# Both halves of a doubling stage asked for before its evictions, in the block inverse of a hybrid layer

## The chip, the cores and the metric

One Trainium2 chip, one core, one launch. The metric is the device time of the whole kernel in microseconds; the kernel before has a median of 1342.84 us over three runs (1340.01 to 1342.85).

The engines are named as in the profile: PE is TensorE (matmuls), PEld its weight loads, DVE VectorE, ACT ScalarE, POOL GpSimd, SP SyncE, whose queue issues most DMAs. L1113 means line 1113 of the kernel before.

## The reference, cut to what matters

A transformer layer over 512 tokens of width 1024: a projection, two sequence mixers (A: gated delta rule with 8 heads; B: retention with 4 heads), an output projection and an MLP. The change lies in mixer A. There, for each head and each chunk of tokens, the inverse of a unit lower triangular matrix is needed:

```
lower = jnp.where(strict, jnp.einsum('bhncd,bhnmd->bhncm', k_beta, k) * decay, 0.0)
eye = jnp.broadcast_to(jnp.eye(CHUNK, dtype=jnp.float32), lower.shape)
t_inv = lax.linalg.triangular_solve(lower, eye, left_side=True, lower=True, unit_diagonal=True)
u = jnp.einsum('bhncm,bhnme->bhnce', t_inv, v * beta[..., None])
w = jnp.einsum('bhncm,bhnmd->bhncd', t_inv, k_beta * jnp.exp(g_cum)[..., None])
...
def step(state, inp):
    qe, ww, uu, aqk, kd, ld = inp
    v_new = uu - jnp.einsum('bhck,bhkv->bhcv', ww, state)
    o = jnp.einsum('bhck,bhkv->bhcv', qe, state) + jnp.einsum('bhcm,bhmv->bhcv', aqk, v_new)
    state = state * ld[..., None, None] + jnp.einsum('bhck,bhcv->bhkv', kd, v_new)
    return state, o
```

## The kernel before, in words

Most of the kernel is large matrix products in three terms (weights and activations are each split into a high and a low part). Weights come by DMA into a `raw` tile, ACT makes the high part `whi` (L148) and DVE the low part `wlo` (L149); then PE multiplies.

The kernel uses chunks of 128 tokens for mixer A, so there are 8 heads x 4 chunks = 32 triangular blocks of 128 x 128. They are inverted in two steps.

*Base inverse* (`base_inverse`, L1032). The 32 x 32 diagonal blocks of all 32 matrices are inverted by substitution on DVE. ACT then copies these inverses to their places in `rt` in eight copies (L1077) and one copy within `rn` (L1071). `rn` holds the inverses in one orientation, `rt` in the other.

*Doubling* (`double_blocks`, L1080). It makes 64 x 64 inverses out of pairs of 32 x 32 ones, then 128 x 128 out of 64 x 64. The 32 matrices are two groups of 16. A 32 x 32 pair has two corners, at partitions 0 to 63 and 64 to 127 (`pairs`).

- Stage 1 (`first`) multiplies a block of the matrix (`mt`, a view of the tile `acc`) by `rn`, into a PSUM bank for each group (`p1`); the result is evicted to `ys` (a view of the tile `mrb`), which stage 2 reads.
- Stage 2 (`left`, `right`) multiplies `ys` by `rt`, into a bank for each group (`p2`); the result is evicted, negated, to `rt` and to `rn`. `rn` is read by the third stage, `rt` by the stages from the fourth on.
- The third and fourth products work on 64 x 64 blocks in quarters of the set, and the change leaves them alone.

In each of the first two stages a loop over q issues one corner of group 0 abreast with the other corner of group 1 (L1110, L1118; in stage 2 also one `right` product), then the evictions of these corners, then the next q. The evictions of stage 1 are L1113 on DVE for group 0 and L1114 on ACT for group 1; those of stage 2 are L1123 (ACT) and L1125 (DVE) into `rt`, and L1127, on DVE for both groups, into `rn`. Each matmul here is float32, and the profile shows two PE records (and two weight loads) for it: 64 in a half of stage 1, 96 in a half of stage 2. PSUM banks come from a pool of three under the tag `dl`.

The order of PE's work is fixed by hand: a planner (`Clock`, L659) interleaves "chains" (dependent work such as the doubling) with "fillers" (the large products). A chain gives the planner a pause with `yield`, in microseconds of the planner's own clock; until it is due, fillers are placed, in units of three matmuls of 0.227 us each by the planner (L753 to L758). Every matmul goes through L668 and keeps program order. After the doubling the event "doubled" is done, and four recurrences follow, which hand over between PE and ACT or DVE in each of four chunks. `DB_US` is 1.2. The order on the other engines is set by a scheduler, by priorities; the evictions here have `KEY_PRIO` (600), the splits of weights in this phase `AHEAD` (700), L1077 has 0.

SP issues the loads of weights; some loads are followed by copies and accumulating DMAs (L135, by POOL) that prepare sums of weight blocks in DRAM for later.

Of the kernel before, what the change touches and what calls it, by code (L numbers as in the profile page):

```python
# [15 lines left out]
ALU = mybir.AluOpType  # L16
# [13 lines left out]
SMALL_US, CONV_US, TOK_US, PK_US, INV_US, DB_US = 10.5, 6.5, 2.5, 2.0, 46, 1.2  # L30
VT_US, KS_US, PX_US, PC_US, GATE_US, FEAT_US, INV_PRIO, CONV_PRIO, SMALL_PRIO, KEY_PRIO, DECAY_US, AHEAD, TR_US, REC_PRIO, OUT_PRIO, SUM_PRIO = 2.5, 2.4, 3.5, 2.4, 11.0, 1.0, 0, 600, 800, 600, 20.0, 700, 2.2, 900, 900, 300
# [32 lines left out]
def hybrid_block_kernel(ctx: ExitStack, tc: tile.TileContext, a: dict, out: bass.AP):  # L64
    nc = tc.nc
# [379 lines left out]
    def two_halves(pool, name, tag, n, width):  # L445
        return Halves(n, [
            pf.tile([P, 2048], F32, tag=tag, name=name)[:, : n * width].rearrange("p (n w) -> p n w", n=n),
            pool.tile([P, n, width], F32, name=name),
        ])
# [5 lines left out]
    rt = two_halves(pa, "rt", "f2", 16, P)  # L455
# [6 lines left out]
    with tc.tile_pool(name="xp", bufs=2) as xp:  # L462
# [105 lines left out]
        hi, lo = kept[0]  # L568
# [359 lines left out]
    def acc_rows(t, half):  # L928
        return acc_t[:, t, half * 512 : half * 512 + 512]
# [54 lines left out]
    with delta_rule:  # L984
# [95 lines left out]
        def double_blocks():  # L1080
            groups = [(m0, slice(m0, m0 + 16), rn_all[0][:, m0 : m0 + 16, :]) for m0 in (0, 16)]
            ys = [rn_all[1][:, h, :].rearrange("p (n c) -> p n c", n=16) for h in (1, 0)]
            pairs = [(slice(b, b + 32), slice(b + 32, b + 64)) for b in (0, 64)]

            def bank(n):
                return psx.tile([P, T], F32, tag="dl", name="dl", bufs=3).rearrange("p (n c) -> p n c", n=n)

            def abreast(*streams):

                for step in zip(*streams):  # L1090
                    before = clock.now
                    for args in step:
                        clock.matmul(*args, start=True, stop=True)
                    clock.now = before + (clock.now - before) / len(streams)

            def first(g, q, p):
                (m0, _, rn), (lo, hi) = groups[g], pairs[q]
                return [(p[hi, n, :], mt[lo, m0 + n, hi], rn[lo, n, 0:32]) for n in range(16)]

            def left(g, q, p):  # L1100
                (m0, _, _), (lo, hi) = groups[g], pairs[q]
                return [(p[lo, n, :], ys[g][hi, n, 0:32], rt[hi, m0 + n, hi]) for n in range(16)]

            def right(g, p):
                m0, hi = groups[g][0], pairs[0][1]
                return [(p[hi, n, :], rt[hi, m0 + n, hi], ys[g][hi, n, 0:32]) for n in range(16)]

            p1 = [bank(16) for _ in range(2)]
            for q in range(2):
                abreast(first(0, q, p1[0]), first(1, 1 - q, p1[1]))  # L1110
                with tc.high_priority(KEY_PRIO):
                    hi0, hi1 = pairs[q][1], pairs[1 - q][1]
                    nc.vector.tensor_copy(ys[0][hi0, :, 0:32], p1[0][hi0])  # L1113
                    nc.scalar.copy(ys[1][hi1, :, 0:32], p1[1][hi1])  # L1114
            yield 1.5 * DB_US
            p2 = [bank(16) for _ in range(2)]
            for q in range(2):
                abreast(left(0, q, p2[0]), left(1, 1 - q, p2[1]), right(q, p2[q]))  # L1118
                with tc.high_priority(KEY_PRIO):
                    for g, (lo, hi) in ((0, pairs[q]), (1, pairs[1 - q])):  # L1120
                        dst = rt[lo, groups[g][1], hi]
                        if g:
                            nc.scalar.mul(dst, p2[g][lo], -1.0)  # L1123
                        else:
                            nc.vector.tensor_scalar(dst, p2[g][lo], -1.0, None, ALU.mult)  # L1125
                    hi = pairs[0][1]
                    nc.vector.tensor_scalar(groups[q][2][hi, :, 0:32], p2[q][hi], -1.0, None, ALU.mult)  # L1127
            yield 1.5 * DB_US
            lo, hi = slice(0, 64), slice(64, 128)
            units = [(g, slice(8 * i, 8 * i + 8)) for g in range(2) for i in range(2)]  # L1130

            def third(u, p):
                g, ns = units[u]
                m0, _, rn = groups[g]
                return [(p[hi, n - ns.start, :], mt[lo, m0 + n, hi], rn[lo, n, :]) for n in range(ns.start, ns.stop)]

            def fourth(u, p):
                g, ns = units[u]
                m0 = groups[g][0]
                return [(p[lo, n - ns.start, :], ys[g][hi, n, :], rt[hi, m0 + n, hi]) for n in range(ns.start, ns.stop)]  # L1140

            def keep_third(u, p):
                g, ns = units[u]
                with tc.high_priority(KEY_PRIO):
                    nc.vector.tensor_copy(ys[g][hi, ns], p[hi])

            def keep_fourth(u, p):
                g, ns = units[u]
                m0 = groups[g][0]
                with tc.high_priority(KEY_PRIO):  # L1150
                    nc.scalar.mul(rt[lo, m0 + ns.start : m0 + ns.stop, hi], p[lo], -1.0)

            for u in range(2):
                p = bank(8)
                abreast(third(u, p))
                keep_third(u, p)
            yield 1.5 * DB_US
            for u in range(2):
                p3, p4 = bank(8), bank(8)
                abreast(third(2 + u, p3), fourth(u, p4))  # L1160
                keep_third(2 + u, p3)
                keep_fourth(u, p4)
                yield 1.5 * DB_US
            for u in range(2, 4):
                p = bank(8)
                abreast(fourth(u, p))
                keep_fourth(u, p)
            yield 1.5 * DB_US
            clock.done("doubled")
# [268 lines left out]
        def delta_chain():  # L1438
            yield "inverse"
            yield from double_blocks()  # L1440
            for g2 in range(4):
                for f in range(4):
                    yield f"v{g2}{f}"
                yield f"q{g2}"
                yield from recurrence(g2)
                clock.start(gate_chain(g2))
                if g2 == 1:
                    feature_sums()
# [55 lines left out]
    with tc.tile_pool(name="pb", bufs=1) as pb_:  # L1504
# [129 lines left out]
        for h in range(4):  # L1634
# [13 lines left out]
            else:  # L1648
                for half, pss in branch_partial(w_br[1], og, 4 * (h - 1)):
                    for t in range(4):  # L1650
                        dst = acc_rows(t, half)
# [381 lines left out]
```

## Time and profile before

| what | value |
|---|---|
| median of three runs | 1342.84 us |
| profiled execution | 1337.54 us |
| its span, first to last instruction | 1335.8 us |
| DVE busy | 70% |
| ACT busy | 50% |
| mean granted PE clock | 0.992 |

The profile is of one execution, so sums are made against its 1337.54 us, of which 1335.8 are the span. Rows of the timeline give start and length in us, engine, line, operation, the tile written and those read, and in brackets the idle time before the group and what released it. In rows of stretches each engine has its busy time and its count of instructions; PEclk is the share of the PE clock that was granted. "issue" is idle time for which the profile knows no releaser.

### The profile page before, as it was taken

Reading aid. Unit: us, or ns where it says so; the run is one execution under the profiler, and the core shown is the slowest. Engines: PE = TensorE matmul, PEld = TensorE weight load, DVE = VectorE, ACT = ScalarE, POOL = GpSimd, SP = SyncE. Lnnn points to the kernel's source line nnn. Section 1 sums busy time; section 2 is a strip of 40 time slices with the busy share of each in tenths; the row PEclk is TensorE's granted clock in tenths of the full one; section 3 lists DMA queues with packets and bytes.
Section 4 is the critical chain, followed back from the end, with each engine's and each line's share of the span. In section 5 each row is a group of like instructions: output and inputs, shape, how many; then the busy total and the mean of one; then the engine's idle time right before and its main releaser. Section 6 shows DMA issues by size and latency. Waiting matters only on the chain.

```text
span 1335.8 us, 17525 instructions
## 1 busy us (share of the span) xinstructions
PE 1310.9 (98%) x6591; PEld 1089.5 (82%) x6591; DVE 930.7 (70%) x1561; ACT 668.0 (50%) x1167; POOL 90.4 (7%) x95
## 2 busy tenths in 40 slices
PE   9999799999999999999999999999999999999997
PEld 7888588888888878888888888888889888888786
DVE  6889556676567568987577766889675746647478
ACT  5784345555534434554453353455356636355364
POOL 2101100000010001000000000000001010000001
PEclk9999799999999999999999999999999999999999
DMA  5436935366766658896394282455629796848835
GB/s 192 132 110 158 190 80 126 95 146 177 191 166 159 139 158 172 248 290 137 76 274 112 80 239 77 134 169 175 231 77 236 224 250 172 252 130 228 230 116 136
DMA packets 115557, 223.16 MB, mean 167 GB/s; under 512 B 6982, under 2 KB 38896, under 8 KB 114960
## 3 DMA queue, kind: packets, MB, share of 16 engines
q1 hardware_dynamic: 96496, 175.13, 41.2%
q0 software_dynamic: 16944, 40.54, 18.6%
q10 hardware_dynamic: 2032, 6.36, 1.3%
q8 instruction: 52, 0.85, 0.3%
q14 instruction: 33, 0.27, 0.1%
HBM read 216.75 MB, written 72.37 MB: 216 GB/s over the span
## 4 chain that ended last, share of the span: by engine, by line
PE 86%; DVE 6%; ACT 4%; DMA 2%; issue 1%; DVEq 0%; ACTq 0%
PE mm L668 17%; PE mm L317 17%; PE dl L317 11%; PE mm L93 10%; PE mm L94 10%; PE mm L95 10%; PE dl L668 6%; PE tr L397 1%; DVE wlo L149 1%; PE dl L94 1%; PE dl L95 1%; PE dl L93 1%; PE tr L677 1%; DMA raw<-sums 1%; PE mm L632 1%
## 5 line engine op out<-in xcount | busy, mean ns | idle before, releaser
L149 DVE TENSOR_TENSOR wlo<-raw,whi 128x1024 fp32r<-128x1024 f32 x269 | 328.2, 1222 | 210.4 <-ACT whi L148 206.2
L148 ACT CAST whi<-raw 128x1024 fp32r<-128x1024 f32 x269 | 282.4, 1052 | 358.2 <-PE mm L317 73.1
L668 PE MATMUL mm<-actT,whi 128*128 128x512 f32 x448 | 145.9, 407 | 0.0
L317 PE MATMUL mm<-whi,xsum 128*128 128x512 f32 x384 | 120.6, 390 | 0.0
L95 PE MATMUL mm<-hn,wlo 128*128 128x512 f32 (+1 forms) x288 | 105.4, 366 | 0.0
L94 PE MATMUL mm<-hn,whi 128*128 128x512 f32 (+1 forms) x288 | 105.3, 366 | 0.0
L93 PE MATMUL mm<-hn,whi 128*128 128x512 f32 (+1 forms) x288 | 105.3, 366 | 0.0
L668 PEld LDWEIGHTS mm<-actT,whi 128*128 128x128 f32 x448 | 82.7, 192 | 15.5
L668 PE MATMUL mm<-actT,wlo 128*128 128x512 f32 x224 | 88.9, 397 | 0.0
L317 PEld LDWEIGHTS mm<-whi,xsum 128*128 128x128 f32 x384 | 71.8, 188 | 14.9
L317 PE MATMUL mm<-wlo,xsum 128*128 128x512 f32 x192 | 74.8, 390 | 0.0
L317 PE MATMUL dl<-whi,ffq 128*128 128x512 f32 x224 | 71.2, 389 | 0.0
L668 PE MATMUL mm<-whi,og 128*128 128x512 f32 x192 | 62.7, 398 | 0.0
L93 PEld LDWEIGHTS mm<-hn,whi 128*128 128x128 f32 x288 | 54.3, 189 | 8.8
L94 PEld LDWEIGHTS mm<-hn,whi 128*128 128x128 f32 x288 | 54.3, 189 | 8.7
L95 PEld LDWEIGHTS mm<-hn,wlo 128*128 128x128 f32 x288 | 54.3, 189 | 8.6
L317 PE MATMUL dl<-whi,actT 128*128 128x512 f32 x192 | 61.2, 390 | 0.0
L668 PE MATMUL mm<-whi,actT 128*128 128x512 f32 x176 | 59.9, 403 | 1.0 <-DVE qf L906 1.0
L317 PE MATMUL mm<-whi,ffq 128*128 128x512 f32 x192 | 60.9, 389 | 0.0
L135 POOL DMA_DIRECT2D sums<-in_w_in_dram x28 | 32.6, 1164 | 386.9 <-DMA sums<-in_w_in_dram 386.9
L1826 DVE TENSOR_TENSOR ffq<-r,ffq 128x512 fp32r<-128x512 f32 (+1 forms) x64 | 39.1, 620 | 28.1 <-ACT ffq L1826 27.9
L93 PE MATMUL mm<-actT,whi 128*128 128x512 f32 x128 | 51.5, 403 | 0.0
(393 smaller groups left out, 2840.9 us busy)
## 6 DMA issues: line engine op xcount, KB each, us to landing
raw<-in_w_in_dram SPq DMA_DIRECT2D x95, 512.0 KB, 4.8
raw<-sums SPq DMA_DIRECT2D x64, 512.0 KB, 4.2
raw<-in_w_up_dram SPq DMA_DIRECT2D x36, 512.0 KB, 7.0
sums<-in_w_in_dram SPq DMA_DIRECT2D x32, 512.0 KB, 5.3
sums<-in_w_down_dram SPq DMA_DIRECT2D x32, 512.0 KB, 6.4
sums<-in_w_in_dram POOLq DMA_DIRECT2D x28, 512.0 KB, 7.2
raw<-in_w_down_dram SPq DMA_DIRECT2D x24, 512.0 KB, 4.5
sums<-sums POOLq DMA_DIRECT2D x20, 512.0 KB, 8.1
```

The lines of the kernel that those rows point to most:

```text
L93: nc.tensor.matmul(ps, lh, rh, start=first, stop=False)
L94: nc.tensor.matmul(ps, lh, rl, start=False, stop=False)
L95: nc.tensor.matmul(ps, ll, rh, start=False, stop=last)
L135: tc.keep_in_program_order(nc.gpsimd.dma_start(dst, src, accum_op=ALU.add))
L148: nc.scalar.copy(hi[:, :n], raw[:, :n])
L149: nc.vector.tensor_tensor(lo[:, :n], raw[:, :n], hi[:, :n], ALU.subtract)
L317: m = nc.tensor.matmul(pss[t], lhs[i // 2], rhs[i % 2], start=first and k + i == 0, stop=k + i == 5, skip_group_check=not first,)
L397: nc.tensor.transpose(ps, src, ident)
L632: pin(nc.tensor.matmul(first_keys[f][:, 256:512], ws[w][:, kk, :], xs[x][:, 2 * j + kk, 256:512], start=False, stop=kk == 1 and i == 2, sk ...
L668: m = tc.keep_in_program_order(nc.tensor.matmul(*args, **kwargs))
L677: tc.keep_in_program_order(nc.tensor.transpose(ps, src, ident if by is None else by))
L1826: return nc.scalar.copy(dst[0], r), nc.vector.tensor_tensor(dst[1], r, dst[0], ALU.subtract)
```

## The change

In stages 1 and 2 the matmuls of both values of q are now issued before any eviction. The evictions follow, four in stage 1 and six in stage 2; DVE takes all of group 0, ACT all of group 1 (before, DVE also evicted the `rn` part of group 1). In stage 2 the `rn` evictions come first. The two pauses are 2.0 instead of 1.5 times `DB_US`.

```diff
             p1 = [bank(16) for _ in range(2)]
             for q in range(2):
                 abreast(first(0, q, p1[0]), first(1, 1 - q, p1[1]))
-                with tc.high_priority(KEY_PRIO):
-                    hi0, hi1 = pairs[q][1], pairs[1 - q][1]
-                    nc.vector.tensor_copy(ys[0][hi0, :, 0:32], p1[0][hi0])
-                    nc.scalar.copy(ys[1][hi1, :, 0:32], p1[1][hi1])
-            yield 1.5 * DB_US
+            with tc.high_priority(KEY_PRIO):
+                for _, hi in pairs:
+                    nc.vector.tensor_copy(ys[0][hi, :, 0:32], p1[0][hi])
+                    nc.scalar.copy(ys[1][hi, :, 0:32], p1[1][hi])
+            yield 2.0 * DB_US
             p2 = [bank(16) for _ in range(2)]
             for q in range(2):
                 abreast(left(0, q, p2[0]), left(1, 1 - q, p2[1]), right(q, p2[q]))
-                with tc.high_priority(KEY_PRIO):
-                    for g, (lo, hi) in ((0, pairs[q]), (1, pairs[1 - q])):
-                        dst = rt[lo, groups[g][1], hi]
-                        if g:
-                            nc.scalar.mul(dst, p2[g][lo], -1.0)
-                        else:
-                            nc.vector.tensor_scalar(dst, p2[g][lo], -1.0, None, ALU.mult)
-                    hi = pairs[0][1]
-                    nc.vector.tensor_scalar(groups[q][2][hi, :, 0:32], p2[q][hi], -1.0, None, ALU.mult)
-            yield 1.5 * DB_US
+            with tc.high_priority(KEY_PRIO):
+                hi = pairs[0][1]
+                nc.vector.tensor_scalar(groups[0][2][hi, :, 0:32], p2[0][hi], -1.0, None, ALU.mult)
+                nc.scalar.mul(groups[1][2][hi, :, 0:32], p2[1][hi], -1.0)
+                for lo, hi in pairs:
+                    nc.vector.tensor_scalar(rt[lo, groups[0][1], hi], p2[0][lo], -1.0, None, ALU.mult)
+                    nc.scalar.mul(rt[lo, groups[1][1], hi], p2[1][lo], -1.0)
+            yield 2.0 * DB_US
```

## The prediction

> **What bounds the kernel now.** The page comes first.
>
> ```profile
> span 1335.8 us, 17525 instructions
> ...
> PE 1310.9 (98%) x6591; PEld 1089.5 (82%) x6591; DVE 930.7 (70%) x1561; ACT 668.0 (50%) x1167; POOL 90.4 (7%) x95
> ...
> PEclk9999799999999999999999999999999999999999
> ...
> q8 instruction: 52, 0.85, 0.3%
> ```
>
> TensorE (PE) is busy for 1310.9 of 1335.8 us, so only 24.9 us of the span can come from its idle time; its clock dips in one slice of the forty, the fifth (134 to 167 us). Next, who PE waits for over the whole run (us in total, times, longest):
>
> ```profile
> PE dl L668 <- DVE mrb L1113: 3.4, 1, 3.4
> PE dl L668 <- issue: 3.1, 1, 3.1
> PE dl L668 <- DVE rn L1127: 2.4, 1, 2.4
> ...
> PE dl L668 <- ACT mrb L1114: 0.7, 1, 0.7
> ```
>
> Those four are 9.6 us, all of them on the matmuls of the doubling. Third, stretches of the span, cut where the granted clock changes (length; PE, PEld, DVE, ACT, POOL busy with counts; PEclk; DMA share; GB/s):
>
> ```profile
> 144.10:147.51 3.41, 0.79 (x50) 0.67 (x43) 2.17 (x6) 2.87 (x5) 0.85 (x1) 1.00 1.06 330
> 147.51:150.92 3.41, 1.89 (x61) 1.75 (x63) 0.69 (x2) 2.96 (x6) 0.00 (x0) 0.50 0.91 92
> 150.92:154.34 3.42, 3.42 (x19) 2.68 (x14) 0.70 (x1) 1.38 (x3) 0.72 (x2) 0.50 0.94 233
> 154.34:157.75 3.41, 1.77 (x99) 1.29 (x97) 2.80 (x4) 1.55 (x3) 2.36 (x3) 1.00 1.02 219
> 157.75:161.17 3.42, 1.80 (x86) 1.67 (x87) 0.71 (x2) 0.17 (x1) 0.05 (x1) 0.50 1.06 132
> ...
> 164.58:167.99 3.41, 3.41 (x10) 2.18 (x8) 0.64 (x1) 0.37 (x1) 0.00 (x0) 0.50 0.25 47
> 167.99:171.40 3.41, 3.41 (x39) 3.12 (x39) 2.00 (x3) 1.26 (x2) 0.00 (x0) 1.00 0.00 0
> ...
> 185.00:250.00 65.00, 65.00 (x323) 54.97 (x321) 43.88 (x93) 36.19 (x101) 4.54 (x4) 1.00 0.50 112
> ```
>
> A stretch in which PE was busy for 0.79 or 1.77 of 3.41 us is followed by one at half clock (0.50); one busy throughout is followed by one at full clock. After the doubling PE has no gap: 65.00 of 65.00 us. So time that PE gains here is not waited for again soon.
>
> The doubling itself, PE alone (start, us, ..., idle before and its releaser):
>
> ```profile
> 140.19 0.61 PE L668 MATMUL mm<-actT,whi 128*128 128x512 f32 x2
> 140.87 0.61 PE L668 MATMUL mm<-actT,whi 128*128 128x512 f32 x2
> ...
> 143.68 1.20 PE L668 MATMUL dl<-rn,acc 32*32 32x32 f32 x64
> 148.29 0.31 PE L668 MATMUL dl<-rn,acc 32*32 32x32 f32 x2 [3.41 <-DVE mrb L1113]
> 149.34 1.91 PE L668 MATMUL dl<-rn,acc 32*32 32x32 f32 x62 [0.74 <-ACT mrb L1114]
> ...
> 152.63 1.05 PE L668 MATMUL mm<-actT,whi 128*128 128x512 f32 x2
> ...
> 153.91 0.83 PE L668 MATMUL mm<-actT,whi 128*128 128x512 f32 x2
> ...
> 154.90 0.22 PE L668 MATMUL dl<-rt,mrb 32*32 32x32 f32 x2
> ...
> 155.92 0.19 PE L668 MATMUL dl<-mrb,rt 32*32 32x32 f32 x1
> 158.53 0.26 PE L668 MATMUL dl<-rt,mrb 32*32 32x32 f32 x2 [2.42 <-DVE rn L1127]
> ...
> 163.45 0.20 PE L668 MATMUL dl<-rt,mrb 32*32 32x32 f32 x1 [3.12 <-issue]
> ...
> 167.94 2.08 PE L668 MATMUL dl<-rn,acc 64*64 64x64 f32 x32
> ```
>
> The second half of each stage waits for the evictions of the first half, although the two halves touch other partitions: as I read it, a write to a PSUM bank is held back by a reader of that bank. The halves are 143.68 and 148.29 in stage 1, 154.90 and 158.53 in stage 2; the third stage starts at 167.94. Filler matmuls run at 0.68 us per three at full clock (140.19 to 140.87) and 1.28 at half (152.63 to 153.91), 0.227 and 0.427 each.
>
> **The change part by part.** The same matmuls and as many evictions; nothing is removed but the two turn-rounds, and no DMA is in what moves.
>
> Stage 1. Its second 64 matmuls follow the first at once: 1.20 us more, 144.88 to 146.1. The 3.41 and 0.74 us of waits go. The pause asked for rises from 1.5 to 2.0 times 1.2 us; fillers come three at a time, so nine (2.04 us by the planner) become twelve (2.72): 146.1 to 148.8. They are useful work done sooner and cost nothing.
>
> What is late next is the evictions that stage 2 reads. On VectorE (DVE) and ScalarE (ACT), before:
>
> ```profile
> 146.29 1.23 DVE L149 TENSOR_TENSOR wlo<-raw,whi 128x1024 fp32r<-128x1024 f32 x1 [1.12 <-ACT whi L148]
> 147.55 0.68 DVE L1113 COPY mrb<-dl 32x512 f32<-32x512 f32 x1
> ...
> 146.29 2.40 ACT L1077 COPY rt<-mrb 32x512 f32<-32x512 f32 x4
> 148.71 0.58 ACT L1114 COPY mrb<-dl 32x512 f32<-32x512 f32 x1
> 149.32 1.24 ACT L1077 COPY rt<-mrb 32x512 f32<-32x512 f32 x2
> ...
> 163.82 0.69 DVE L1125 TENSOR_SCALAR rt<-dl 32x512 f32<-32x512 f32 x1 [5.34 <-PE dl L668]
> 164.54 0.68 DVE L1127 TENSOR_SCALAR rn<-dl 32x512 f32<-32x512 f32 x1
> ```
>
> DVE stands behind a weight split until 147.55 and then has two copies: done by 148.9. ACT had the copies of the base inverse (L1077) ahead of its eviction. In their old place its two evictions are 148.71 + 2 x 0.58 = 149.9; behind all three copies left, 151.7; I take two ahead (the second half lasts 1.20 us, two copies are 1.24): stage 2 starts at 151.1. PE then idles 2.3 us, and behind the waiting matmul stand all later fillers, since PE's order is fixed.
>
> Stage 2. PE is busy only 1.3 us of the stretch 147.51 to 150.92, less than the 1.77 that was followed by half clock, so I take half clock from 150.92, and full clock again from 154.34, since PE fills that stretch but for 0.2 us. The chain of waits has both paces of what follows:
>
> ```profile
> 158.53 1.80 PE dl L668 x86
> ...
> 163.87 4.14 PE mm L668 x9
> ```
>
> At half clock a small matmul costs 1.80 / 86 = 20.9 ns, at full clock 12.6 (96 from 154.90 to about 156.1). So 155 of the 192 are done by 154.34. The 2.42 us wait goes. The 3.12 us "issue" remains to be placed. PE's own instructions come in blocks on q8: 0.85 MB / 52 = 16 KB, and 2 x 6591 / 52 = 253 recorded PE instructions (matmul and weight load) a block. In 160.1 to 163.5 us the DMA queues show one such block, amid the accumulating DMAs of q0, with the queues full:
>
> ```profile
> q0 software_dynamic: 289, 0.56, 103.6%
> q8 instruction: 1, 0.02, 4.2%
> ```
>
> I read the stall as PE out of instructions. It came after 96 + 86 = 182 of the 192 matmuls. Three more fillers stand ahead now, so it comes about three sooner in the stage, after 179: 24 x 0.0126 past 154.34, at 154.64. Bounds: nothing (the block is there), or until 163.45 as before (the block goes out no sooner). I take 3.12 again, nearest to the one such row: resumed at 157.76, just as the stretch of the stall sets half clock again, and 13 x 0.0209 ends the stage at 158.0.
>
> [...]
>
> The evictions of stage 2: the three on DVE take 0.68 + 2 x 0.69 = 2.06 us, with ACT's three beside them, instead of four on DVE. The third stage reads rn, which is first; its second bank is that of DVE's three. Twelve fillers (2.72 us at least) cover 2.06. With six more fillers, part of the next weight tile is asked for sooner, so its ACT and DVE split may come first: 1.23 more on DVE, 3.3 in all, covered at half clock, 0.6 us late at full.
>
> Fillers: half clock until the first stretch PE fills has ended, 161.17: 3.17 / 0.427 = 7.4 of them, then 4.6 x 0.227 = 1.0: the third stage starts at 162.2, 5.7 us before 167.94, with six more fillers done (6 x 0.227 = 1.4). **The sum is -7.1 us.** The profiled execution took 1337.54 us (span 1335.8 and 1.7 around it), the runs' median is 1342.84. 1330.4 against 1337.54, carried to the median, is 1335.7 us. The eviction bounds (149.9, 151.7) move this by -1.2 and +0.6; at 149.9 the stage is also partly at full clock, about a microsecond more. The forecast's own range reaches halfway to the rivals A and B below: 1333.3 to 1338.9.
>
> **The rivals.** (A) *The block is pinned.* The fetch waits for q0's traffic, which PE does not drive, and lands when it did: PE stands from 154.64 to 163.45, ends at 163.75, has half clock to 167.99 (9.9 fillers) and starts the third stage at 168.5: 0.6 later, less 1.4 of fillers, a gain of 0.8: 1342.0 us. For it: q0 at 103.6%. Against: nothing shows when the block was asked for, and PE now asks sooner.
>
> (B) *No stall.* The block is there, and PE, busy from 151.1, has full clock from 154.34. The last 37 matmuls run at 12.6 ns: end 154.8, twelve fillers to 157.5; 10.4 + 1.4 = 11.8 us gained, 1331.0. [...] For it: PE stalls like this nowhere else. Against: no denser stretch of instructions exists before, and this one becomes denser.
>
> (C) *Slower.* The planner places everything after "doubled" by its own clock, and that is now six fillers further on. The four recurrences hand over between PE and DVE or ACT 11 times each, 44 in all; before they cost PE nothing (65.00 of 65.00). If the shift puts a weight split or conv ahead of the awaited eviction, at 0.25 us each on average that is 11 us, 3.9 more than the gain: 1346.7. It decides from 7.1 / 44 = 0.16 us each. Against: due times move with the clock, by the same constants.
>
> **How the numbers follow.** Forecast 0.66, A 0.12, B 0.12, C 0.10. A measurement tells about 0.2%, 2.7 us, from no change. The forecast and B are faster but for 0.01, so faster 0.77, same 0.13 (A and that remainder), slower 0.10. The range takes in B's centre and A, 1330.5 to 1342.5; C and B's far half are left out.
>
> **What would show it.** Right: PE's waits for L1113 and for L1127 gone; 128 small matmuls without a break from about 143.7; one wait before stage 2, for ACT L1114, of 1 to 3 us; a later start at "issue" within the last 20 matmuls of stage 2; the third stage near 162; PE full from there on. Wrong: an "issue" wait over 6 us (A) or none (B); "issue" waits elsewhere; PE waits of tenths in the recurrences (C); evictions behind a conv on DVE, which would start stage 2 after 153.

## The result, and the profile after

The changed kernel has a median of 1330.74 us over eight executions (1327.59 to 1332.4), the kernel before 1338.71 over eight (1334.78 to 1342.85). The ratio is 0.9934, with a 95% interval of 0.9913 to 0.9956. It is faster, by 0.44 to 0.87%. The two highest executions of the kernel before were among the three from which the prediction took 1342.84. The profiled execution of the changed kernel took 1331.12 us, 6.4 less than the 1337.54 before.

The head of the page and the row of the granted clock, after:

```profile
span 1329.3 us, 17523 instructions
...
PE 1308.2 (98%) x6591; PEld 1088.1 (82%) x6591; DVE 931.4 (70%) x1560; ACT 668.0 (50%) x1168; POOL 89.7 (7%) x95
...
PEclk9999899999999999999999999999999999999999
```

The span is 6.5 us shorter with 2.7 us less busy time: most of the gain is idle time of PE, the rest matmuls that no longer ran at half clock (10.2 us of it instead of 6.8 + 10.2, below). Who PE waits for, over the whole run:

```profile
PE dl L668 <- issue: 4.3, 1, 4.3
...
PE dl L668 <- ACT mrb L1114: 1.0, 1, 1.0
```

Of the four waits before (9.6 us) the two for DVE are gone, ACT's is 1.0, and "issue" has grown from 3.1 to 4.3: 5.3 us in all. PE in the doubling:

```profile
143.79 2.21 PE L668 MATMUL dl<-rn,acc 32*32 32x32 f32 x128
...
148.88 0.24 PE L668 MATMUL dl<-rt,mrb 32*32 32x32 f32 x2
150.10 0.21 PE L668 MATMUL dl<-rt,mrb 32*32 32x32 f32 x1 [0.98 <-ACT mrb L1114]
...
156.80 0.25 PE L668 MATMUL dl<-mrb,rt 32*32 32x32 f32 x1 [4.31 <-issue]
...
162.29 2.07 PE L668 MATMUL dl<-rn,acc 64*64 64x64 f32 x32
```

Stage 1 is one run of 128 matmuls in 2.21 us; before, its halves began 4.6 us apart. The third stage starts at 162.29 instead of 167.94. The same on ACT, then on DVE (L1121 is now the eviction into `rn`, L1124 one into `rt`; L1113 and L1114 have kept their numbers):

```profile
146.42 2.43 ACT L1077 COPY rt<-mrb 32x512 f32<-32x512 f32 x4
148.87 1.18 ACT L1114 COPY mrb<-dl 32x512 f32<-32x512 f32 x2
...
150.66 1.74 ACT L1077 COPY rt<-mrb 32x512 f32<-32x512 f32 x3
```

```profile
147.69 1.41 DVE L1113 COPY mrb<-dl 32x512 f32<-32x512 f32 x2
...
157.26 0.68 DVE L1121 TENSOR_SCALAR rn<-dl 32x512 f32<-32x512 f32 x1 [4.14 <-PE dl L668]
157.97 1.38 DVE L1124 TENSOR_SCALAR rt<-dl 32x512 f32<-32x512 f32 x2
```

ACT's two evictions stand together, ahead of the three copies of L1077 that are left. DVE is done with stage 2 at 159.35, well before the third stage. The chain that ended last counts the matmuls on either side of the "issue" wait, called the stall from here on:

```profile
150.10 2.39 PE dl L668 x177
152.49 4.31 issue
156.80 0.47 PE dl L668 x13
157.26 5.10 PE mm L668 x12
```

PE stops after 2 + 177 = 179 of the 192 matmuls of stage 2. The stretches, cut again where the clock changes:

```profile
147.81:151.61 3.80, 2.82 (x149) 2.24 (x149) 2.03 (x4) 3.69 (x7) 0.00 (x0) 1.00 0.96 106
151.61:155.03 3.42, 0.88 (x54) 0.75 (x43) 1.47 (x2) 1.42 (x3) 0.90 (x2) 0.50 0.93 245
155.03:158.44 3.41, 1.64 (x16) 1.39 (x17) 1.15 (x2) 1.11 (x2) 1.67 (x2) 0.50 1.04 210
158.44:161.85 3.41, 3.41 (x9) 2.64 (x9) 1.65 (x3) 2.27 (x4) 0.56 (x1) 0.50 1.00 129
161.85:165.27 3.42, 3.42 (x38) 2.86 (x38) 1.74 (x3) 0.00 (x0) 0.00 (x0) 1.00 1.07 193
```

There is one stay at half clock, 10.2 us from 151.61 to 161.85, where before there were two, 6.8 and 10.2 us. Between 185 and 250 us PE has no gap, as before:

```profile
185.00:250.00 65.00, 65.00 (x328) 55.30 (x327) 44.15 (x103) 37.16 (x105) 3.40 (x3) 1.00 0.43 105
```

### The profile page after: what moved, and what is told of

Its sections match the earlier page's. It is cut to its first block, busy times and chain, and to the rows that moved or that the text cites. A ratio compares the mean times of both kernels' runs of the same rounds, so it can differ in the third digit from the quotient of the medians.

```text
span 1329.3 us, 17523 instructions
## 1 busy us (share of the span) xinstructions
PE 1308.2 (98%) x6591; PEld 1088.1 (82%) x6591; DVE 931.4 (70%) x1560; ACT 668.0 (50%) x1168; POOL 89.7 (7%) x95
## 4 chain that ended last, share of the span: by engine, by line
PE 84%; DVE 7%; ACT 4%; DMA 2%; issue 2%; DVEq 0%; ACTq 0%
PE mm L668 17%; PE mm L317 16%; PE mm L95 10%; PE mm L93 10%; PE mm L94 10%; PE dl L317 9%; PE dl L668 6%; DVE wlo L149 2%; PE tr L397 1%; PE dl L94 1%; PE dl L95 1%; PE dl L93 1%; PE tr L677 1%; DMA raw<-in_w_up_dram 1%; PE mm L632 1%
## 5 line engine op out<-in xcount | busy, mean ns | idle before, releaser
L668 PE MATMUL mm<-actT,whi 128*128 128x512 f32 x448 | 145.3, 406 | 0.0
L668 PEld LDWEIGHTS mm<-actT,whi 128*128 128x128 f32 x448 | 82.5, 191 | 15.5
L668 PE MATMUL mm<-actT,wlo 128*128 128x512 f32 x224 | 88.4, 395 | 0.0
L668 PE MATMUL mm<-whi,og 128*128 128x512 f32 x192 | 62.4, 397 | 0.0
L668 PE MATMUL mm<-whi,actT 128*128 128x512 f32 x176 | 60.4, 405 | 1.0 <-DVE qf L906 1.0
```

The lines of the kernel that those rows point to most:

```text
L668: m = tc.keep_in_program_order(nc.tensor.matmul(*args, **kwargs))
```

## The experiments

The theory: PE's instructions come in blocks (16 KB on q8, 253 recorded instructions each); the next block is asked for near the start of stage 2, which is a guess of mine, since no record shows it, and its arrival sets the end of stage 2. Removing waits ahead of stage 2 then moves the end, removing a wait inside it does not. The rivals: the waits simply add up; and the stall belongs to the work of stage 2 (clock, semaphore, PSUM), not to instructions.

| kernel | median us | ratio to before, 95% interval |
|---|---|---|
| the change | 1330.74 | 0.9934 (0.9913 to 0.9956) |
| the change, timed again | 1329.51 | 0.9951 (0.9931 to 0.9970) |
| stage 1 alone | 1328.81 | 0.9946 (0.9929 to 0.9963) |
| stage 2 alone | 1335.64 | 0.9997 (0.9980 to 1.0013) |
| pauses left at 1.5 | 1330.30 | 0.9959 (0.9942 to 0.9977) |
| 24 fillers inside stage 2 | 1326.89 | 0.9928 (0.9909 to 0.9948) |
| 15 fillers inside stage 2 | 1324.67 | 0.9915 (0.9895 to 0.9935) |
| 180 instructions more at the start | 1323.73 | 0.9905 (0.9885 to 0.9925) |
| 72 instructions more at the start | 1333.00, one execution | |
| DMA jobs later | 1332.15, one execution | |

**Stage 1 alone.** The lines of the change up to the first pause; stage 2 as before, evictions inside the loop.

```diff
             for q in range(2):
                 abreast(first(0, q, p1[0]), first(1, 1 - q, p1[1]))
-                with tc.high_priority(KEY_PRIO):
...
-            yield 1.5 * DB_US
+            with tc.high_priority(KEY_PRIO):
+                for _, hi in pairs:
...
+            yield 2.0 * DB_US
```

Expected:

> Only stage 1 is changed; stage 2 and its pause are as before. Theory 1 (after the first waits are gone, the end of stage 2 is set by the arrival of a block of PE instructions, asked for as PE runs into stage 2): the 2.4 us wait for DVE between the halves of stage 2 stays, the issue wait shrinks to 1 to 2.5 us, stage 2 ends within 1 us of the changed kernel's 157.2, and the time is within 2 us of the changed kernel's: ratio to before 0.993 to 0.996. Theory 2 (the waits simply add): the issue wait stays at 3 to 4.3 us, stage 2 ends near 159.5 to 160, ratio 0.9965 (4.2 us of waits and half a microsecond of clock).

Measured: 0.9946. The waits of PE in its doubling, from the timeline of PE:

```profile
149.73 0.21 PE L668 MATMUL dl<-rt,mrb 32*32 32x32 f32 x1 [0.95 <-ACT mrb L1114]
...
154.07 0.26 PE L668 MATMUL dl<-rt,mrb 32*32 32x32 f32 x2 [3.15 <-DVE rn L1127]
...
156.44 0.26 PE L668 MATMUL dl<-mrb,rt 32*32 32x32 f32 x1 [0.66 <-issue]
```

PE waits 3.15 us for DVE in the middle of stage 2, and then only 0.66 for "issue", less than I had put down. It resumes at 156.44, where the changed kernel resumes at 156.80. By the theory, the time that the wait for DVE takes is time that the block needed anyway. The intervals of this kernel and of the whole change overlap.

**Stage 2 alone.** The other half of the change.

```diff
             for q in range(2):
                 abreast(left(0, q, p2[0]), left(1, 1 - q, p2[1]), right(q, p2[q]))
-                with tc.high_priority(KEY_PRIO):
...
-            yield 1.5 * DB_US
+            with tc.high_priority(KEY_PRIO):
+                hi = pairs[0][1]
...
+            yield 2.0 * DB_US
```

Expected:

> Only stage 2 is changed; stage 1 is as before. Theory 1 (block of instructions): stage 2 starts at about 154.9 as before, the wait for DVE goes, the issue wait grows from 3.1 to 5 or 6 us, the stage ends at about 163 as before; gain 0 to 1.5 us: ratio 0.999 to 1.000. Theory 2 (the waits add): the issue wait stays near 3.1, the stage ends near 161, gain 2.5 to 4 us, ratio 0.997 to 0.998.

Measured: 0.9997, no change. The chain that ended last:

```profile
155.51 2.16 PE dl L668 x182
157.67 5.62 issue
163.29 0.43 PE dl L668 x8
```

The wait of 2.42 us for DVE is gone and "issue" has grown by 2.5, from 3.12 to 5.62. PE resumes at 163.29, before at 163.45. The theory that the waits add would have had it near 161; it falls.

**180 instructions more at the start.** The first eight warming matmuls at the start of the kernel become 98 small ones; nothing reads their result. The edit is one line longer, so L668 is L669 here.

```diff
-        keep_warm(8)
+        for _ in range(98):
+            tc.keep_in_program_order(nc.tensor.matmul(pw[0:32, 0:64], warm[:, 0:32], warm[:, 0:64], start=True, stop=True))
```

Expected, of one execution first:

> The changed kernel with the first 8 warming matmuls at its start replaced by 98 small ones (90 more matmuls, 180 more PE instructions; the result they write is never read). [...] If the wait belongs to the work itself (the clock, a semaphore, PSUM), it stays at about the 179th matmul of stage 2 with 3 to 4.5 us.

and then timed:

> The kernel with 180 more PE instructions at its start, now timed. Block theory: 4.3 us of the issue wait and about 1.5 us of half clock less than the changed kernel, so ratio to before 0.989 to 0.991. If its one time of 1323.4 us was luck, 0.993 to 0.996.

Measured: 1323.40 us in the one execution, then a median of 1323.73 and a ratio of 0.9905. The chain of the first:

```profile
150.08 2.21 PE dl L669 x190
152.29 4.53 PE mm L669 x12
156.83 2.00 PE dl L669 x32
```

Stage 2 starts as in the changed kernel, runs its 190 matmuls without a stop, and the third stage starts at 156.83, 5.5 us sooner than at 162.29. The profile among the timed executions does have an "issue" wait, in the third stage:

```profile
152.07 2.94 PE mm L669 x12
155.01 0.84 PE dl L669 x12
155.85 1.17 issue
```

So the stall is made shorter and moved, not removed for good. It comes after 13 + 12 + 12 = 37 more matmuls than in the changed kernel; by the 253 recorded instructions a block from q8, the end of the next block would lie 253 - 180 = 73 instructions, 36 to 37 matmuls, past the old place. In the first execution the same twelve fillers took 4.53 us, 0.38 each, between the 0.227 of full clock and the 0.427 of half, and no wait is seen.

**72 instructions more at the start.** 44 small matmuls in place of 98.

```diff
-        keep_warm(8)
+        for _ in range(44):
+            tc.keep_in_program_order(nc.tensor.matmul(pw[0:32, 0:64], warm[:, 0:32], warm[:, 0:64], start=True, stop=True))
```

> Control: the first 8 warming matmuls replaced by 44 small ones, 72 more PE instructions. Block theory: the place where PE runs out moves up by 36 matmuls, to about the 143rd of the 192 in stage 2, and the issue wait is there again, 4 to 5 us; the time is the changed kernel's. If the small matmuls at the start and not the block's place took the wait away, there is none here either, and the time is near 1323.

Measured, in the chain:

```profile
151.37 1.70 PE dl L669 x141
153.07 4.16 issue
```

The "issue" wait comes after 2 + 141 = 143 of the 192, as put down. The one execution took 1333.00 us, 1.1 more than the highest of the changed kernel's six beside it; its stage 2 also began 1.3 us later than the 150.10 above. So the small matmuls alone do not take the stall away, and its place in the work is not fixed; it goes by the count of instructions. The count can be read directly. These are the stretches from the start of the span to a time inside the stall (the first count is of matmuls, the second of weight loads), first before the change:

```profile
0.00:162.50 162.50, 149.04 (x1108) 124.82 (x1109) 128.85 (x350) 99.83 (x241) 23.80 (x28) 0.96 0.58 157
```

after it:

```profile
0.00:156.00 156.00, 146.90 (x1108) 123.05 (x1108) 127.42 (x348) 98.97 (x240) 21.81 (x27) 0.99 0.56 157
```

stage 1 alone:

```profile
0.00:156.20 156.20, 147.69 (x1108) 123.63 (x1108) 128.79 (x350) 99.61 (x241) 21.93 (x27) 0.99 0.57 159
```

and with 44 small matmuls at the start:

```profile
0.00:156.50 156.50, 147.14 (x1108) 124.77 (x1108) 127.85 (x348) 99.15 (x240) 21.44 (x27) 0.99 0.55 156
```

Each kernel stops with 1108 matmuls and 1108 or 1109 weight loads begun, at four times and three places of the program. The other profiles that stop in stage 2 (stage 2 alone, DMA jobs later, pauses at 1.5, the change timed again) have the same counts. With 180 instructions more, the later stall stands at 1235 matmuls and 1236 weight loads, 255 recorded instructions further on, about one block of 16 KB (253 by the count on q8). And in all nine profiles with an "issue" wait in the doubling, a block is recorded on the instruction queue q8 between 2.2 and 3.3 us before PE goes on: at 160.15 us before the change, where PE resumes at 163.45, and at 154.6 after it, where PE resumes at 156.80. So PE has run out of instructions; that the stall belongs to the work of stage 2 is ruled out.

The count says where PE can run out, not that it will. With 180 instructions more, PE passes its 1108th matmul at 151.0 us, in the middle of stage 2, and does not stop; with 24 fillers inside stage 2 it passes it at 157.4, again without a stop. There a block is recorded on q8 at 146.8 and at 154.8, that is 4.2 and 2.6 us ahead of the need; in the changed kernel PE stops at 152.5, and the block is recorded at 154.6. So in those two kernels the record stands ahead of the need, and in the changed one 2.1 us behind it. When a block is asked for is in no record.

**The DMA jobs later.** The copies and accumulating DMAs for the block sums begin at 175 us of the planner's clock.

```diff
-JOBS_FROM, JOB_US = 70.0, 8.5
+JOBS_FROM, JOB_US = 175.0, 8.5
```

> The changed kernel with the copies and accumulating DMAs for the later block sums started at 175 us of the planner's clock, not at 70 (the same work, later), so that q0 and the copies are silent in the doubling. If the block is late because the DMA queues are full, the issue wait falls from 4.3 to 0.5 to 2.5 us. If it is late by a fixed latency of its own, the wait stays at 3.5 to 4.5 us. The whole time may be longer, since the sums are made later; it is not what this run is for.

Measured, in the chain:

```profile
149.87 2.08 PE dl L668 x177
151.95 2.17 issue
154.12 0.34 PE dl L668 x13
```

The stall is half as long at the same place. The DMA queues from 146 to 154 us (packets, MB, share of the 16 engines), in this kernel:

```profile
q1 hardware_dynamic: 528, 0.52, 23.8%
q8 instruction: 1, 0.02, 1.1%
```

and in the changed kernel:

```profile
q0 software_dynamic: 144, 0.52, 58.4%
q1 hardware_dynamic: 651, 0.87, 34.8%
q8 instruction: 1, 0.02, 0.7%
```

The q8 rows are of different blocks: in the changed kernel the record stands at 147, and the block that PE waits for comes after these eight microseconds, at 154.6; here the block that it waits for is recorded at 151.2. From the start of stage 2 to the resumption it is 154.12 - 149.87 = 4.25 us here, 6.70 in the changed kernel, 6.63 when that was timed again, 6.71 with stage 1 alone, 7.78 with stage 2 alone and 8.55 before. With 72 instructions more, where the block ends 36 matmuls sooner in stage 2, it is 5.86. By this one execution, the copies and adds make about 2.4 us of the 6.70. All of it lies ahead of the record on q8, which stands 1.3 us after the start of stage 2 here and 4.5 us after it in the changed kernel; which of the two queues holds the block up is open. The whole time of this kernel says nothing on that, since the sums are made later.

**Other work during the wait.** In the changed kernel, a pause between the halves of stage 2, so that fillers run while the block comes: 5.4 us (24 fillers), then 3.4 (15).

```diff
                 abreast(left(0, q, p2[0]), left(1, 1 - q, p2[1]), right(q, p2[q]))
+                if q == 0:
+                    yield 5.4
```

> The changed kernel with a pause of 5.4 us of the planner's clock (24 more fillers) between the halves of stage 2. Block theory: PE asks for the block in the first half as before and has 5.4 us of other work until it arrives near 157, so the issue wait falls to 0 to 1 us and the clock stays up; the third stage starts near 161 with 24 fillers more done: 5 to 7 us less than the changed kernel, ratio to before 0.988 to 0.991. Rival (the doubling's end is what counts, since four recurrences follow it): the recurrences start 24 fillers later and the time is that of the changed kernel or up to 3 us more, ratio 0.994 to 0.997.

Measured: 0.9928, less of a gain than put down, though in the doubling all went as expected:

```profile
149.96 1.20 PE dl L668 x94
151.16 5.68 PE mm L668 x24
156.84 1.14 PE dl L668 x96
157.97 1.59 PE mm L668 x6
...
160.69 2.00 PE dl L668 x32
```

There is no stall, and full clock throughout (24 fillers in 5.68 us). The third stage is at 160.69, with 24 - 3 = 21 more fillers done (nine instead of twelve before the third stage), worth 4.8 us. Some of it is given back later; PE's waits between 185 and 400 us:

```profile
PE tr L677 <- DVE og L1420: 1.2, 1, 1.2
PE dl L668 <- DVE qf L906: 0.8, 1, 0.8
```

The shorter pause:

> As the kernel with 24 fillers between the halves of stage 2, but a pause of 3.4 us (15 fillers). Block theory: PE runs out near 155.5 and the block arrives near 156.5, an issue wait of 0.5 to 1.5 us; the recurrences start 9 fillers sooner, so the waits of 1.2 and 0.8 us seen there with 24 fillers may go: ratio to before 0.990 to 0.994. Rival (any pause there costs as much as it gains): 0.994 to 0.996.

Measured: 0.9915. There is no "issue" wait, where I had put down 0.5 to 1.5 us: from 154.49 to 157.03 us the fillers ran at 0.42 us each, the pace of half clock, and the 15 took 5.25 us, about as long as the 24 above. Between 185 and 400 us there is one wait of PE, 0.8 us for ACT. That the shorter pause is the better one is not shown: the intervals overlap.

**The pauses left at 1.5.** The change without its two longer pauses.

```diff
-            yield 2.0 * DB_US
+            yield 1.5 * DB_US
```

> The changed kernel with the two pauses left at 1.5 times. Theory: the pauses are worth little, since PE's wait for ACT before stage 2 grows by what the fillers shrink (1.0 to about 1.7 us) and the block sets the end of stage 2 all the same: ratio to before within 0.001 of the changed kernel's in its own call, 0.994 to 0.996. Rival (the longer pauses are a part of the gain, as cover for the evictions): 0.997 to 0.999.

Measured: 0.9959; PE waits 1.4 us for ACT before stage 2 and 4.1 for the block. The interval overlaps with that of the change, so the longer pauses are worth little at most.

The changed kernel was also timed again, beside the kernels with 24 fillers and with 98 small matmuls:

> The changed kernel once more, beside the others of this call: ratio to before 0.993 to 0.996 by every theory; an issue wait of 3.5 to 5 us after about 179 matmuls of stage 2.

Measured: 0.9951, with an "issue" wait of 4.54 us after 2 + 177 matmuls. Against that, the version with 180 more instructions is 5.8 us faster, the lowest median of all; its stage 2 begins at 149.85 us, that of the changed kernel at 149.81, so its gain doesn't come from the start of the kernel. The one with 15 fillers, timed beside other executions of the kernel before, takes its gain without any work that is thrown away.

## Why the prediction was right or wrong

**The step that failed is the last one of the sum**: "carried to the median, is 1335.7 us". The base, 1342.84, stood on three executions, two of which turned out the highest of eight. On the median of the eight, 1338.71, the same -7.1 us gives 1331.6, and on the profile's own time it gave 1330.4; measured were 1330.74 and, in the profile, 1331.12. The 1337.54 of the profile should have warned that 1342.84 was high. The range, 1330.5 to 1342.5, was made around that base too and held the time only just. That the sum of -7.1 us itself comes so near to the measured change is luck in part: four of its terms were mis-sized, and they cancel, as the next paragraphs show.

**Stage 1** was right: the waits of 3.41 and 0.74 us are gone, the second half takes 1.0 us more, and this is where the gain comes from, the whole of it as far as the intervals can tell. Stage 1 alone gives 0.9946. Whether the wait for a reader of the same PSUM bank is needed by the chip or only set by the program's order was not tested.

**The start of stage 2** was mis-sized. I took 151.1, with two copies of L1077 ahead of ACT's evictions; the evictions kept their old place, the lower of my two bounds, and PE went on at 150.10. The wait was 0.98, not 2.3.

**Stage 2** was booked wrongly. I let its 2.42 us go as a gain and put the stall back at the length it had. The length is not a property of the stall: in the kernels with the DMA jobs in place PE went on 5.9 to 8.6 us after stage 2 began, and what it didn't wait for in between it waited for at the end. So "issue" was 4.31, not 3.12, and the rewriting of stage 2, the larger part of the diff, is worth nothing by itself that the measurement shows (0.9997, interval 0.9980 to 1.0013). The place, after 179 matmuls, was right, because it was counted in instructions.

**The errors cancel, by luck.** The start of stage 2 was put 1.0 us too late; its first 179 matmuls took 2.39 us where I had 3.54, since the clock fell later; the stall was 1.2 us longer than put; and from the resumption to the third stage it took 5.5 us where I had 4.4, since the half clock lasted longer. So the third stage was put at 162.2 and came at 162.29, with six more fillers done, as forecast; from there to the end 0.5 us of the 7.0 is not found again in the span.

**The clock** was half right. It fell once, not twice, and was back at 161.85 where I had 161.17. I had it fall at 150.92, by the 1.3 us of work in the stretch before; the stretches had shifted, and it fell at 151.61, after a stretch with 2.82 us of work in 3.80.

**The evictions** of stage 2 cost nothing, as forecast: done at 159.35, fillers until 162.3.

**The rivals.** A, the block pinned to the DMA traffic, is wrong as told: with stage 2 begun 4.8 us sooner, PE went on 6.7 us sooner. But the traffic does lengthen the wait, by about 2.4 us in the one execution without it. B, no stall, did not happen by itself and did when the end of the block was moved: the third stage at 156.83, where B had 157.5. In the changed kernel, where the small matmuls of stage 2 stand closer together than before, PE stood still for 4.31 us, before for 3.12. C, waits in the recurrences, did not happen in the changed kernel (65.00 of 65.00 us busy). With 24 fillers moved ahead of "doubled" there were 2.0 us of waits behind it, 0.8 of them on a matmul of a recurrence.

## What to carry to other kernels

A wait that is removed may be waited for again at the next arrival, as the 2.42 us for DVE were here, so time each half of a change by itself: one half was all of the gain (0.9946) and the other none (0.9997). When PE stands still at "issue" in a burst of small matmuls, count the instructions it has begun in two kernels; here the count was the same, 1108 matmuls, at three places of the program, and a block was recorded on the instruction queue 2.2 to 3.3 us before PE went on, which told that it was out of instructions. 24 long matmuls put into the burst (5.68 us) covered the wait for the block here; a denser burst did not (4.31 us at "issue"). And take the base of a forecast from more than three executions, or from the one whose trace is read.

## What the runs showed of the hardware that had not been expected

The burst of small matmuls in stage 2 outran the supply of PE instructions: 177 recorded matmuls of 32 x 32 took 2.39 us, and PE went on with the block that it then lacked only 6.70 us after the burst began, 4.25 with fewer DMAs in the queues. The stall moved with the count of instructions from the very start of the program: 36 more small matmuls at the start moved it up by 36 matmuls at 150 us, and 90 more took it out of the stage and 5.8 us off the kernel. The next stall stood 255 recorded instructions behind the first, and PE went on 2.2 to 3.3 us after the record of a block on q8.

A stretch of 3.80 us in which PE was busy for 2.82 was followed by half clock, so three quarters of the time were not enough here to keep it up. That is no threshold: with 24 fillers inside stage 2, the same wait of 1.0 us ahead of stage 2 was followed by full clock (PEclk 1.00 from 143 to 165 us).
